# All eleven chunk pairs of the feed-forward layer in seven products, spaced token tile steps, first input chunk in two transfers

## The chip, the core and the metric

The kernel runs on one core of a Trainium2 chip. The metric is the device time of one execution in microseconds (us). Matrix products run on TensorE (PE in the profile; its weight loads are PEld), elementwise work on VectorE (DVE), ScalarE (ACT) and GpSimd (POOL), and transfers are issued from the queues of SyncE (SP), ScalarE and GpSimd. All five run side by side and wait for one another through semaphores; each works through its own instructions in order.

## The reference

A decoder trunk of two layers on 1024 tokens of width 1024, in float32. Each layer adds a mixer (layer 0: dilated attention and forgetting attention side by side; layer 1: differential attention) and then a convolutional gated feed-forward part to the running sum `h`. The part that the change touches most:

```python
def conv_glu_ffn(n, w_up, conv_w, conv_b, w_down):   # n: 1024x1024, D_FF = 2816
    gate, up = jnp.split(n @ w_up, 2, axis=-1)
    gp = jnp.pad(gate, ((0, 0), (CONV_WIDTH - 1, 0), (0, 0)))
    conv = conv_b
    for j in range(CONV_WIDTH):
        conv = conv + gp[:, j:j + s] * conv_w[j]
    return (jax.nn.silu(conv) * up) @ w_down
...
h = h + conv_glu_ffn(rms_norm(h, ffn_norm[l]), ...)
...
return rms_norm(h, final_norm)
```

## The kernel before

Everything is kept transposed: channels lie on the 128 partitions, tokens along the free dimension, in two halves of 512 tokens (`HT`). A float32 product is made of three products of a rounded-down type (`mm3`): each operand is split into a high and a low part (`split`, `wget`), and high x high, high x low and low x high are summed in PSUM. So one "block product" (512 input channels or one 128-channel chunk with four output tiles, 512 tokens) is 12 matmuls of 128x512, or 24 of half the width.

**Feed-forward, up.** The 2816 inner channels are 22 chunks of 128 (`NF`). For each chunk `ffn_up` makes gate and up with Winograd's form of Strassen's scheme, in seven block products (numbered 1 to 7 in `step`) where the plain way has eight. Weight sums for it are made on GpSimd (`plan_ffn`).

**Feed-forward, down.** The down product takes the chunks in pairs (2j, 2j+1). A pair with two output halves (tiles 0 to 3 and 4 to 7) and two token halves is again a 2x2 block product. For the last ten pairs (`NS = 10`) it is done in seven products: the sums of the activations (`td`, four per pair) are made by `close` in `ffn_up` on VectorE, the sums of the weights (`sd`, four per pair) by `sums` on GpSimd, one pair per chunk from chunk 10 (`NH`) on; both go to DRAM and are read back. The first pair is done plainly, in eight products. `ffn_down` runs through the parts that `down_parts` lists: each part is a row of items, an item is one weight tile and one activation tile (two loads, two splits, one block product), and all items of a part are summed in one set of four PSUM banks, `X` or `Y`. There are eight parts with 10, 12, 10, 10, 12, 10, 12 and 2 items, 78 in all. At the end of a part `take` adds the banks to the residual tiles `h`, and where the part is marked done, `after` starts the next norm on them (`after0` in layer 0, `after1` in layer 1). In the last part of layer 1 the last items (`tail`) run in two passes over 256 tokens each, and `after1` calls `finish` (statistics, reciprocal root, spread over the partitions, scaling, output) for each.

**Attention and projections** are woven by `weave`: attention steps are events with planned times, the projections (`jobs`) are generators that yield after each small piece with a cost in planned us. After each event the planner runs the job at hand until its account `done` reaches the event's `goal`. The last job of a mixer is `blocks` in `out_jobs`: nine steps; step m scales token tile m of the first token half (`token_blocks`, VectorE), stores it, and splits tile m-1 (ScalarE, VectorE). Behind each step stand three yields; they run pieces of `rest` (the second token half of the output projection) if the attention unit that it needs is done (`rest.after in self.fins`), and else cost 0.1 each. Afterwards the framework puts each engine's instructions in order by the program's order and by when it reckons them ready.

**Start.** The first 128 input channels (512 KB) come in one transfer on SP's queue behind two weight tiles; `norm_chunk` then works on each token half.

Of the kernel before, what the change touches and what calls it, by code (L numbers as in the profile page):

```python
# [13 lines left out]
ALU = mybir.AluOpType  # L14
# [4 lines left out]
P = 128  # L19
T = 1024  # L20
D = 1024
NK = D // P
HT = 512
NF = 22
# [25 lines left out]
class Trunk:  # L50
# [175 lines left out]
    def norm_a(self, st, c, half, src, gi):  # L226

        nc = self.nc
# [4 lines left out]
        if c == 0:  # L233
            st["acc"][half] = st["acct"](half)
            sq = st["acc"][half]
        else:
            sq = st["sqt"]()
# [3 lines left out]
    def norm_b(self, st, c, half, src, gi, sq):  # L241

        nc = self.nc
# [5 lines left out]
        if c:  # L249
            nc.vector.tensor_tensor(st["acc"][half], st["acc"][half], sq, ALU.add)  # L250
# [582 lines left out]
    NS = 10  # L833
# [47 lines left out]
    def down_parts(self, l):  # L881

        n0 = NF // 2 - self.NS
        A = lambda k, c: self.a["wdown"][l, k][:, c * HT:(c + 1) * HT]
        B = lambda k, t: self.act[l][k][:, t * HT:(t + 1) * HT]
        js = range(n0, NF // 2)
        std = lambda c, t: [(A(k, c), B(k, t)) for k in range(2 * n0)]
# [4 lines left out]
                list(zip(odd(A, 0), odd(B, 0))) + std(0, 0),  # L892
                list(zip(S(2), Tk(2))),
                list(zip(S(3), Tk(3))),
                list(zip(odd(A, 1), Tk(4))) + std(1, 0),
                list(zip(S(1), Tk(1))),
                list(zip(S(4), odd(B, 1))) + std(0, 1),
                std(1, 1)]
# [24 lines left out]
    def ffn_up(self, l, plan, blocks, down):  # L923
# [4 lines left out]
        order, W, _ = plan  # L928
# [69 lines left out]
        def close():  # L998
            tt = nc.vector.tensor_tensor
            while late:  # L1000
# [7 lines left out]
                if j < NF // 2 - self.NS:  # L1008
                    continue
# [16 lines left out]
        def sums(fc, p):  # L1026


            j = NF // 2 - self.NS + fc - self.NH
# [4 lines left out]
            if p == 6:  # L1034
                for x, k, c in (("11", 0, 0), ("21", 0, 1), ("22", 1, 1), ("12", 1, 0)):
                    sw[x] = t()
                    self.put(sw[x], self.a["wdown"][l, 2 * j + k][:, c * HT:(c + 1) * HT])
            elif p == 5:
                tt(sw["11"], sw["11"], sw["21"], ALU.subtract)
                self.store(self.sd[l][j, 3], sw["11"])  # L1040
                nc.gpsimd.dma_start(sw["21"], self.a["wdown"][l, 2 * j + 1][:, HT:], accum_op=ALU.add)
# [39 lines left out]
    def ffn_down(self, l, plan, act, h, after, mid):  # L1081
# [8 lines left out]
        parts = [(X, True, None, False), (X, False, (0, 0), True), (Y, True, (0, 1), False), (Y, False, (4, 1), False),  # L1090
                 (Y, False, (4, 0), True), (X, True, (4, 1), False), (X, False, (0, 1), True), (Y, True, (4, 1), True)]
# [7 lines left out]
        for q, (banks, begin, at, done) in enumerate(parts):  # L1099
            if begin:  # L1100
                ps = [self.pj(t) for t in banks]
            self.pmap["small"] = ["A"] if q == 7 else ["Q"]
            seg = D[q]
            end = len(seg) - min(3, len(seg) - 1)
            lastq = q == 7 and l == 1
# [43 lines left out]
    def run(self):  # L1149
# [29 lines left out]
        def out_jobs(l, w, base):  # L1179
# [24 lines left out]
            def blocks():  # L1204
                rest.fetch()
                more = rest.gen()
                for m in range(9):
# [7 lines left out]
                    for _ in range(3):  # L1215
                        yield next(more, 0.0) if rest.after in self.fins else 0.1
# [69 lines left out]
        for c in range(NK):  # L1286
# [4 lines left out]
            nc.sync.dma_start(xc, a["xT"][c * P:(c + 1) * P, :])  # L1291
# [155 lines left out]
        def after0(m, c):  # L1447
            hf = c.start // HT
            if (m, hf) == (0, 0):
# [69 lines left out]
        def after1(m, c):  # L1519
# [3 lines left out]
            if m == 0:  # L1523
# [139 lines left out]
```

## Time and profile before

| | us |
|---|---|
| three runs, median (lowest to highest) | 2530.19 (2528.14 to 2540.12) |
| the profiled execution | 2523.64 |
| its span, first to last instruction | 2521.9 |
| TensorE busy | 2445.1 |
| VectorE busy | 1976.4 |
| ScalarE busy | 1219.2 |
| GpSimd busy | 702.6 |

The busy time of an engine is the sum of its instructions' times; what is left of the span is time in which the engine had nothing to do or waited. TensorE's instructions overlap by a part (a matmul begins before the one ahead has left the array), so its pace is read from the distance of two starts.

### The profile page before, as it was taken

The page shows a single profiled execution, that of the slowest core. Times are in us where ns is not written, and L with a number is a line of the kernel's source. Part 1 is how long each engine was busy: PE and PEld are TensorE (multiplying, and loading weights), DVE is VectorE, ACT ScalarE, POOL GpSimd, SP SyncE. Part 2 cuts the span into 40 slices and gives each one's busy share as a digit, 9 for nine tenths or more (in the row PEclk, how much of TensorE's full clock was granted, in tenths as well). Part 3 has the DMA queues.
Part 4 walks back from the last instruction along what each step waited for, and adds up shares of the span by engine and source line. Part 5 has one row for each costly group of instructions (what it writes and reads, how often), then busy time and mean ns, then how long its engine had stood idle before and what let it go on. Part 6 is the DMA issues. An engine that isn't in the chain of part 4 may idle for free.

```text
span 2521.9 us, 38243 instructions
## 1 busy us (share of the span) xinstructions
PE 2445.1 (97%) x12511; PEld 2034.3 (81%) x12511; DVE 1976.4 (78%) x3885; ACT 1219.2 (48%) x2443; POOL 702.6 (28%) x930
## 2 busy tenths in 40 slices
PE   8999999999899999999999999999889999999997
PEld 7899898887688888787888888877767888887786
DVE  7778878877988988775666878887888888887655
ACT  5456655555543434453534555555554343445433
POOL 1211112222544665100021111132135366730000
PEclk9999999999999999999999999999999999999998
DMA  5655556756667887664655555586476678856644
GB/s 186 225 168 168 175 166 207 243 201 235 209 190 229 243 253 223 217 219 160 196 194 179 191 166 181 187 284 201 159 256 187 201 242 252 253 184 235 228 136 152
DMA packets 240790, 515.96 MB, mean 205 GB/s; under 512 B 36696, under 2 KB 49616, under 8 KB 240592
## 3 DMA queue, kind: packets, MB, share of 16 engines
q1 hardware_dynamic: 175184, 311.63, 38.9%
q0 software_dynamic: 64832, 201.37, 24.1%
q8 instruction: 99, 1.62, 0.3%
q14 instruction: 99, 0.81, 0.1%
q10 hardware_dynamic: 576, 0.52, 0.1%
HBM read 349.75 MB, written 163.64 MB: 204 GB/s over the span
## 4 chain that ended last, share of the span: by engine, by line
PE 80%; DMA 6%; DVE 6%; issue 4%; ACT 2%; POOL 1%; SPq 0%; ACTq 0%; DVEq 0%; POOLq 0%
PE pj L145 66%; PE D L145 5%; PE O L145 4%; PE T L148 4%; DVE wl L131 1%; PE small L145 1%; DMA wr<-in_wgate 1%; DMA wr<-in_wdown 1%; DMA ar<-act 1%; ACT wh L129 1%; DMA rt<-sr 1%; DMA ar<-td 1%; DVE e L615 1%; DVE bt L166 1%; DVE e L771 0%
## 5 line engine op out<-in xcount | busy, mean ns | idle before, releaser
L145 PE MATMUL pj<-bt,wh 128*128 128x512 f32 x1760 | 552.1, 394 | 7.3 <-DVE bt L166 4.4
L145 PEld LDWEIGHTS pj<-bt,wh 128*128 128x128 f32 x1760 | 330.5, 188 | 85.5 <-DVE bt L166 6.0
L145 PE MATMUL pj<-nh,wh 128*128 128x512 f32 x864 | 354.6, 410 | 17.8 <-ACT nh L232 8.8
L131 DVE TENSOR_TENSOR wl<-wr,wh 128x512 fp32r<-128x512 f32 (+2 forms) x340 | 239.5, 706 | 162.9 <-ACT wh L129 150.8
L145 PE MATMUL pj<-bt,wl 128*128 128x512 f32 x880 | 346.6, 394 | 0.0
L129 ACT ACTIVATE wh<-wr 128x512 fp32r<-128x512 f32 (+2 forms) x340 | 211.6, 624 | 277.4 <-PE pj L145 121.4
L145 PE MATMUL pj<-nl,wh 128*128 128x512 f32 x864 | 343.9, 398 | 0.0
L145 PE MATMUL pj<-nh,wl 128*128 128x512 f32 x864 | 343.2, 397 | 0.0
L131 DVE TENSOR_TENSOR wl<-wq,wh 128x512 fp32r<-128x512 f32 x268 | 274.3, 1025 | 31.9 <-ACT wh L129 31.7
L129 ACT ACTIVATE wh<-wq 128x512 fp32r<-128x512 f32 x268 | 166.8, 628 | 233.8 <-PE pj L145 176.1
L849 POOL TENSOR_TENSOR wq<-wq 128x512 f32<-128x512 f32 x132 | 202.4, 1538 | 213.9 <-DVE wl L131 106.8
L145 PE MATMUL pj<-ah,wh 128*128 128x512 f32 (+1 forms) x628 | 247.7, 395 | 4.8 <-DVE h L1115 3.1
L145 PE MATMUL pj<-al,wh 128*128 128x512 f32 (+1 forms) x628 | 246.0, 392 | 0.0
L145 PE MATMUL pj<-ah,wl 128*128 128x512 f32 (+1 forms) x628 | 245.8, 392 | 0.0
L145 PEld LDWEIGHTS pj<-nh,wh 128*128 128x128 f32 x864 | 164.7, 191 | 51.2 <-ACT sc L956 9.9
L165 ACT ACTIVATE ph<-T 128x512 fp32r<-128x512 f32 (+3 forms) x288 | 139.2, 487 | 129.6 <-PE T L148 127.1
L145 PEld LDWEIGHTS pj<-bt,wl 128*128 128x128 f32 x880 | 165.5, 188 | 39.5
L145 PEld LDWEIGHTS pj<-nh,wl 128*128 128x128 f32 x864 | 164.0, 190 | 37.3
L145 PEld LDWEIGHTS pj<-nl,wh 128*128 128x128 f32 x864 | 164.7, 191 | 30.1 <-DVE nl L247 0.5
L166 DVE TENSOR_TENSOR pl<-T,ph 128x512 fp32r<-128x512 f32 (+3 forms) x288 | 157.7, 552 | 34.8 <-ACT ph L165 33.6
L148 PE MATMUL T<-ident,e 128*128 128x128 f32 x864 | 143.2, 275 | 6.8 <-DVE e L771 4.0
L145 PE MATMUL pj<-wh,nh 128*128 128x256 f32 (+1 forms) x512 | 149.2, 293 | 0.0
(494 smaller groups left out, 5297.8 us busy)
## 6 DMA issues: line engine op xcount, KB each, us to landing
wq<-in_wgate SPq DMA_DIRECT2D x88, 256.0 KB, 4.6
wq<-in_wup SPq DMA_DIRECT2D x88, 256.0 KB, 5.6
act<-v POOLq DMA_DIRECT2D x44, 512.0 KB, 3.4
td<-sc POOLq DMA_DIRECT2D x80, 256.0 KB, 4.5
wq<-in_wdown SPq DMA_DIRECT2D x80, 256.0 KB, 4.5
sd<-wq POOLq DMA_DIRECT2D x80, 256.0 KB, 4.3
ar<-td SPq DMA_DIRECT2D x80, 256.0 KB, 3.7
wr<-sd SPq DMA_DIRECT2D x80, 256.0 KB, 2.9
```

The lines of the kernel that those rows point to most:

```text
L129: nc.scalar.activation(hi[:, :n], raw[:, :n], AF.Copy)
L131: nc.vector.tensor_tensor(lo[:, :n], raw[:, :n], f(hi[:, :n]), ALU.subtract)
L145: self.last = self.nc.tensor.matmul(*args, **kw)
L148: self.last = self.nc.tensor.transpose(*args)
L165: nc.scalar.activation(hi, src, AF.Copy)
L166: nc.vector.tensor_tensor(lo, src, f(hi), ALU.subtract)
L615: self.nc.vector.tensor_tensor_reduce(out=e[:, k0:k0 + w], in0=d[:, :w], in1=in1(k0, w), scale=1.0, scalar=init, op0=ALU.add, op1=ALU.min, ...
L849: nc.gpsimd.tensor_tensor(dst, x, y, op)
```

## The change

Six edits belong together: `NS` becomes 11, so that the first pair of chunks is done in seven products like the others. Its activation sums are made in chunks 0 and 1, and the weight sums, one pair per chunk from chunk 10 on, now reach to chunk 20. `down_parts` has seven parts of 11 items, 77 in all; the eighth part is gone. The two halves of the output tiles change places in all of it, so the tiles 4 to 7 of the first token half come first, and the last two parts both use the banks `X`: part 5 ends the tiles 0 to 3 of the second token half, part 6 goes on in the same banks and ends the tiles 4 to 7. The running sum of the norm starts at the tile that comes first. In `blocks` a step whose `rest` may not run yet costs 2.0 once instead of 0.1 three times. The first input chunk comes in two transfers of 256 KB, one for each token half.

```diff
--- before.py
+++ after.py
@@ -230,7 +230,7 @@
             g = self.gn[:, gi * 8 + c:gi * 8 + c + 1]
             st["h"][c, half] = self.big.tile([P, HT], F32R, name="nh", tag="big")
             nc.scalar.activation(st["h"][c, half], src, AF.Copy, scale=g)
-        if c == 0:
+        if half not in st["acc"]:
             st["acc"][half] = st["acct"](half)
             sq = st["acc"][half]
         else:
@@ -246,7 +246,7 @@
             st["l"][c, half] = self.big.tile([P, HT], F32R, name="nl", tag="big")
             nc.vector.scalar_tensor_tensor(st["l"][c, half], src, g, f(st["h"][c, half]),
                                            ALU.mult, ALU.subtract)
-        if c:
+        if sq is not st["acc"][half]:
             nc.vector.tensor_tensor(st["acc"][half], st["acc"][half], sq, ALU.add)
 
     def norm_chunk(self, st, c, half, src, gi):
@@ -830,7 +830,7 @@
     NH = 10
 
 
-    NS = 10
+    NS = NF // 2
 
     def plan_ffn(self, l):
         a, nc = self.a, self.nc
@@ -880,22 +880,19 @@
 
     def down_parts(self, l):
 
-        n0 = NF // 2 - self.NS
-        A = lambda k, c: self.a["wdown"][l, k][:, c * HT:(c + 1) * HT]
+        A = lambda k, c: self.a["wdown"][l, k][:, (1 - c) * HT:(2 - c) * HT]
         B = lambda k, t: self.act[l][k][:, t * HT:(t + 1) * HT]
-        js = range(n0, NF // 2)
-        std = lambda c, t: [(A(k, c), B(k, t)) for k in range(2 * n0)]
+        js = range(NF // 2)
         S = lambda i: [self.sd[l][j, i] for j in js]
         Tk = lambda i: [self.td[l][j, i] for j in js]
         odd = lambda f, i: [f(2 * j + 1, i) for j in js]
         return [[(A(2 * j, 0), B(2 * j, 0)) for j in js],
-                list(zip(odd(A, 0), odd(B, 0))) + std(0, 0),
+                list(zip(odd(A, 0), odd(B, 0))),
                 list(zip(S(2), Tk(2))),
                 list(zip(S(3), Tk(3))),
-                list(zip(odd(A, 1), Tk(4))) + std(1, 0),
+                list(zip(odd(A, 1), Tk(4))),
                 list(zip(S(1), Tk(1))),
-                list(zip(S(4), odd(B, 1))) + std(0, 1),
-                std(1, 1)]
+                list(zip(S(4), odd(B, 1)))]
 
     def ffn_order(self):
 
@@ -1005,8 +1002,6 @@
                 tt(x[:, h1], y[1], s.pop((fc, 3)), ALU.mult)
                 self.store(self.act[l][fc], x)
                 j = fc // 2
-                if j < NF // 2 - self.NS:
-                    continue
                 if fc % 2 == 0:
                     t1[0] = scratch()
                     tt(t1[0], x[:, h1], x[:, h0], ALU.subtract)
@@ -1026,7 +1021,7 @@
         def sums(fc, p):
 
 
-            j = NF // 2 - self.NS + fc - self.NH
+            j = fc - self.NH
             if fc < self.NH or j >= NF // 2:
                 return
             tt = nc.gpsimd.tensor_tensor
@@ -1034,11 +1029,11 @@
             if p == 6:
                 for x, k, c in (("11", 0, 0), ("21", 0, 1), ("22", 1, 1), ("12", 1, 0)):
                     sw[x] = t()
-                    self.put(sw[x], self.a["wdown"][l, 2 * j + k][:, c * HT:(c + 1) * HT])
+                    self.put(sw[x], self.a["wdown"][l, 2 * j + k][:, (1 - c) * HT:(2 - c) * HT])
             elif p == 5:
                 tt(sw["11"], sw["11"], sw["21"], ALU.subtract)
                 self.store(self.sd[l][j, 3], sw["11"])
-                nc.gpsimd.dma_start(sw["21"], self.a["wdown"][l, 2 * j + 1][:, HT:], accum_op=ALU.add)
+                nc.gpsimd.dma_start(sw["21"], self.a["wdown"][l, 2 * j + 1][:, :HT], accum_op=ALU.add)
             elif p == 7:
                 tt(sw["22"], sw["22"], sw["11"], ALU.subtract)
                 self.store(self.sd[l][j, 2], sw["22"])
@@ -1087,8 +1082,8 @@
         X, Y = ("A", "A", "B", "O"), ("S", "S", "Q", "Q")
         s0, n = [], 0
 
-        parts = [(X, True, None, False), (X, False, (0, 0), True), (Y, True, (0, 1), False), (Y, False, (4, 1), False),
-                 (Y, False, (4, 0), True), (X, True, (4, 1), False), (X, False, (0, 1), True), (Y, True, (4, 1), True)]
+        parts = [(X, True, None, False), (X, False, (4, 0), True), (Y, True, (4, 1), False), (Y, False, (0, 1), False),
+                 (Y, False, (0, 0), True), (X, True, (0, 1), True), (X, False, (4, 1), True)]
 
         def residual(m0, hf):
             for m in range(m0, m0 + 4):
@@ -1099,10 +1094,10 @@
         for q, (banks, begin, at, done) in enumerate(parts):
             if begin:
                 ps = [self.pj(t) for t in banks]
-            self.pmap["small"] = ["A"] if q == 7 else ["Q"]
+            self.pmap["small"] = ["S"] if q == 6 else ["Q"]
             seg = D[q]
             end = len(seg) - min(3, len(seg) - 1)
-            lastq = q == 7 and l == 1
+            lastq = q == 6 and l == 1
 
             def take(m, c):
 
@@ -1212,8 +1207,11 @@
                         hl = (self.big.tile([P, HT], F32R, name=x, tag="big") for x in ("nh", "nl"))
                         st["h"][m - 1, 0], st["l"][m - 1, 0] = hl
                         self.split(st["h"][m - 1, 0], st["l"][m - 1, 0], t0[m - 1])
-                    for _ in range(3):
-                        yield next(more, 0.0) if rest.after in self.fins else 0.1
+                    if rest.after in self.fins:
+                        for _ in range(3):
+                            yield next(more, 0.0)
+                    else:
+                        yield 2.0
                 while rest.after not in self.fins:
                     yield 0.1
                 yield from more
@@ -1288,7 +1286,8 @@
                 xc = f(ap.tile([P, T], F32R, name="KS", tag="KS", bufs=self.kbufs))
             else:
                 xc = ap.tile([P, T], F32, name="e", tag="e", bufs=self.ebufs)
-            nc.sync.dma_start(xc, a["xT"][c * P:(c + 1) * P, :])
+            for o in cs if c == 0 else [slice(0, T)]:
+                nc.sync.dma_start(xc[:, o], a["xT"][c * P:(c + 1) * P, o])
             for half in range(2):
                 self.norm_chunk(st, c, half, xc[:, cs[half]], 0)
             if c in (1, 3):
@@ -1446,7 +1445,7 @@
 
         def after0(m, c):
             hf = c.start // HT
-            if (m, hf) == (0, 0):
+            if (m, hf) == (4, 0):
                 st1["acct"] = st1["sqt"] = lambda half=0: self.fp.tile([P, HT], F32, name="sc", tag="sc",
                                                                        bufs=self.nsc)
             sq = self.norm_a(st1, m, hf, H[0][m, hf], 2)
@@ -1520,7 +1519,7 @@
             hf, w = divmod(c.start, HT)
             o = slice(w, w + c.stop - c.start)
             h = H[1][m, hf][:, o]
-            if m == 0:
+            if m == 4 * (1 - hf):
                 if w == 0:
                     acc[hf] = self.fp.tile([P, HT], F32, name="sc", tag="sc", bufs=self.nsc)
                 nc.scalar.activation(acc[hf][:, o], h, AF.Square)
```

## Rows read from the trace of the kernel before

**Rows 1.** Page, part 1: busy time, share of the span, instructions of each engine.

```profile
PE 2445.1 (97%) x12511; PEld 2034.3 (81%) x12511; DVE 1976.4 (78%) x3885; ACT 1219.2 (48%) x2443; POOL 702.6 (28%) x930
```

**Rows 2.** Waits of TensorE over the span: total us, times, longest us.

```profile
PE pj L145 <- ACT nh L232: 8.8, 1, 8.8
...
PE small L148 <- DVE pl L166: 7.3, 2, 7.1
...
PE pj L145 <- DVE h L1115: 3.1, 4, 1.3
```

**Rows 3.** Windows: busy us (instructions) of PE, PEld, DVE, ACT, POOL; PE clock, DMA share, GB/s.

```profile
672.00:1035.00 363.00, 363.00 (x1565) 294.37 (x1565) 310.96 (x426) 151.55 (x249) 191.55 (x214) 1.00 0.71 221
...
1803.00:1813.00 10.00, 10.00 (x49) 8.43 (x49) 8.78 (x27) 6.56 (x19) 2.01 (x4) 0.79 0.48 155
1813.00:1831.00 18.00, 16.59 (x91) 13.43 (x90) 11.97 (x28) 8.37 (x22) 0.00 (x0) 1.00 0.31 99
...
2268.00:2503.00 235.00, 233.26 (x1022) 188.29 (x1020) 151.91 (x247) 112.01 (x192) 3.24 (x6) 1.00 0.58 193
```

**Rows 4.** Timeline of TensorE in the last part: start us, duration us.

```profile
2491.21 0.40 PE L145 MATMUL pj<-ah,wh 128*128 128x512 f32 x1
2491.45 0.40 PE L145 MATMUL pj<-al,wh 128*128 128x512 f32 x1
...
2500.39 0.28 PE L145 MATMUL pj<-al,wh 128*128 128x256 f32 x1
2500.51 0.28 PE L145 MATMUL pj<-ah,wl 128*128 128x256 f32 x1
```

**Rows 5.** Groups by line and shape: busy us, mean ns, idle before.

```profile
L1022 DVE TENSOR_TENSOR sc<-v,sc 128x512 f32<-128x512 f32 x20 | 29.6, 1478 | 1.7 <-DMA sc<-act 1.6
...
L1017 DVE TENSOR_TENSOR sc<-v,sc 128x512 f32<-128x512 f32 x20 | 13.7, 686 | 0.1
...
L1043 POOL TENSOR_TENSOR wq<-wq 128x512 f32<-128x512 f32 x20 | 32.2, 1612 | 0.0
```

**Rows 6.** Windows of layer 0's up product: chunk 1 closes; chunk 3 closes, with sums.

```profile
700.00:713.00 13.00, 13.00 (x57) 10.52 (x57) 11.82 (x18) 5.26 (x9) 5.04 (x6) 1.00 0.57 179
...
727.00:741.00 14.00, 14.00 (x63) 11.34 (x62) 13.16 (x21) 5.45 (x10) 6.07 (x8) 1.00 0.76 242
```

**Rows 7.** Timeline of VectorE, end of layer 1's attention.

```profile
1793.10 2.08 DVE L1145 SCALAR_TENSOR_TENSOR rt<-rt,gn,rb 128x512 f32<-128x512 f32 x3
...
1802.02 0.69 DVE L166 TENSOR_TENSOR pl<-T,ph 128x512 fp32r<-128x512 f32 x1
...
1810.99 1.29 DVE L771 SCALAR_TENSOR_TENSOR e<-e,cf 128x1024 f32<-128x1024 f32 x1
```

**Rows 8.** Timeline of TensorE, the same stretch.

```profile
1802.76 1.12 PE L148 MATMUL small<-ident,Ra 128*128 128x128 f32 x4 [7.13 <-DVE pl L166]
```

**Rows 9.** Timeline of the start.

```profile
3.86 0.63 ACT L129 ACTIVATE wh<-wr 128x512 fp32r<-128x512 f32 x1 [1.83 <-DMA wr<-in_wqkA]
...
4.81 0.63 ACT L129 ACTIVATE wh<-wr 128x512 fp32r<-128x512 f32 x1 [0.33 <-DMA wr<-in_wqkA]
...
8.06 0.72 ACT L232 ACTIVATE nh<-e,gn 128x512 fp32r<-128x512 f32 x1 [2.62 <-DMA e<-in_xT]
...
8.84 0.80 PE L145 MATMUL pj<-nh,wh 128*128 128x512 f32 x1 [8.84 <-ACT nh L232]
```

**Rows 10.** Timeline of the end.

```profile
2502.31 0.28 PE L145 MATMUL pj<-ah,wl 128*128 128x256 f32 x1
...
2503.63 0.61 PE L145 MATMUL small<-ones,sc 128*128 128x1 f32 x4 [1.05 <-DVE sc L1537]
...
2507.11 1.32 ACT L1530 ACTIVATE sc<-h 128x256 f32<-128x256 f32 x4
...
2507.57 4.00 PE L145 MATMUL small<-ones,sc 128*128 128x1 f32 x18 [0.66 <-ACT sc L1530]
...
2515.11 3.22 DVE L1566 SCALAR_TENSOR_TENSOR y<-h,gn,small 128x256 f32<-128x256 f32 x8 [1.18 <-PE small L145]
```

## The prediction

> **What bounds the kernel.** I began with the busy shares of the page [rows 1]: TensorE works for 97% of the span, the next engine, VectorE, for 78%. So a gain must take matmuls away or close one of the gaps that make up the other 3%. The list of TensorE's waits [rows 2] says which gaps there are: one of 8.8 us that ends with the first product of ScalarE, two of 7.3 us in all (one of them 7.1) behind `pl` on VectorE, four short ones behind `h`. The windows [rows 3] show that the up product of layer 0 has no gap at all (363.00 of 363.00), that the last down product loses 1.7 us of 235, and that the ten us behind the long wait ran at a granted clock of 0.79, a mix of the lower and the higher level. Then I read the timelines at the three places where the edits meet a gap: the end of layer 1's attention [rows 7, 8], the start [rows 9] and the end [rows 10].
>
> **The eighth product.** Before, a layer's down product has 78 items, after it 77; an item is 12 matmuls of 512 columns. Over two layers 24 matmuls go. Their pace is the window's: 363 us for 1565 of them [rows 3], 0.232 us each; two starts in the last part lie as far apart [rows 4]. **24 x 0.232 = 5.6 us less**, and since TensorE is the bound in both down products, all of it is on the path. The tail of the last part had one item in two passes of 256 columns and now has three. That costs nothing: two half-width starts are 0.12 us apart, so two halves take what one whole takes [rows 4].
>
> What the seven products need in return, per layer: four VectorE sums between 686 and 1478 ns [rows 5], so 2.7 to 5.9 us, three GpSimd sums of about 1.61 us (4.8 us), eight stores and six loads of 256 KB. They fall in chunks 0, 1 and 20 of the up product. I cost them at nothing, and the cover is TensorE's own work there: the window in which chunk 1 closes without sums has VectorE busy for 11.82 of 13 us, the one in which chunk 3 closes with the same sums for 13.16 of 14, and TensorE was full in both [rows 6]. Chunk 20 will look like chunks 10 to 19, which lie in the full window [rows 3]. If that cover were gone, at most 5.9 + 4.8 = 10.7 us per layer would come onto the path (the third rival). The sums of the first pair are read back in the third part, tens of us after they are stored, so their transfers wait for nobody. Each layer also saves one item's four splits.
>
> **The order of the parts.** Exchanging the output halves moves the same work. New is only that the finished tiles 0 to 3 of the second token half are followed by a part in the same banks: its first matmuls wait for `take`, and `take` now shares VectorE with the norm. The nearest rows are the waits behind `h`: four, 3.1 us in all, 1.3 at most [rows 2]. The wait could be nothing, since a tail of nine matmuls per tile (2.1 us) gives `take` time; at the other end it is 1.3 us per layer. I take 0.5 per layer, **1 us more** (0 to 2.6). The same change lets the squares of tiles 0 to 3 run a part earlier, off the path as before.
>
> **The token tile steps.** In layer 0 the attention unit that `rest` needs is done before `blocks` begins, by the planner's own order, so both versions yield the same pieces and nothing changes. In layer 1 it is not. I followed the planner's account through the code: `blocks` begins with the account at 249.0, and the marks that follow are 249.3 and 252.3. At 0.1 a yield a step costs 0.3, so all nine steps go out before the second mark is reached. VectorE shows them as one block: from 1793.10 to the `pl` at 1802.02 nearly nothing but token tiles [rows 7]. That `pl` frees the bank for the four transposes of `Ra`, and TensorE stood still for 7.13 us until 1802.76 [rows 8]; over the next ten us the granted clock averaged 0.79 [rows 3].
>
> At 2.0 a step the account passes the same marks thus: step 0 at the first, step 1 at the second, two behind the next row of scores, one and then two more around the last row, and the last two when the unit is done. The planner gives `rest` three pieces before the end of the list in either case, so no matmul moves back. Ahead of that `pl` now stand three VectorE operations of steps 0 and 1, not fourteen. The most that this can give is the whole wait and the lost clock: 7.1 + 10 x (1 - 0.79) = 9.2 us. But VectorE is then the limit: it was busy for 8.78 of the ten us from 1803 on, and the last row's `e` ends at 1812.3 [rows 3, 7]. Of the sixteen operations of the block some three to seven now stand behind that row, at about 0.65 us each: 2 to 4.5 us by which the last unit ends earlier. What TensorE can put into the hole meanwhile is the first two thirds of `rest`, whose inputs are there. The seven late steps also cost VectorE some 9 us further on, where it has 18 - 11.97 = 6.0 us idle [rows 3]; the 3 us that don't fit could make the first block products wait, which is the bound on the other side. So the edit gives between 9.2 less and 3 more; I take **5 us less**, between VectorE's 4.5 and the whole wait, nearer to the first.
>
> SP's queue waits at the store of that unit's statistics row, with the next weights behind it, so those start as much earlier as the unit ends; POOL's queue issues the tile stores in the same order, only wider apart, and the loads of `rest` behind them.
>
> **The first chunk.** TensorE starts at 8.84, when ScalarE has made the first `nh` from 8.06 on [rows 9]; ScalarE was ready from 5.44 (4.81 + 0.63). The two weight tiles of 256 KB ahead of the chunk reached ScalarE at 3.86 and 4.81, 0.95 us apart. A first half of 256 KB at that pace would be there at 5.76: 2.3 us less. If the transfers behind it share the engines evenly, it comes when the whole came: nothing. The second half is needed only after six cold matmuls, and one more issue ahead of the next chunk costs that chunk little, since ScalarE has four operations per chunk to do first. I take **1.5 us less**. The Trainium skill speaks against cutting transfers up: DMA: Bandwidth & Descriptors, section Bandwidth, wants them batched to 1 MiB or more. By the fit that the same page gives for another queue (2.0 us and 436 GB/s) the smaller transfer would be some 0.6 us faster, an estimate by which the sum below would gain 0.9 us less; the weights' rows here come closer together than that.
>
> **The end.** From the start of the last half-width matmul at 2502.31 to the end of the span at 2521.9 are 19.6 us [rows 10]. Before, the second pass of 256 columns was over in 1.4 us, so the statistics of the first pass began only behind it, at 2503.63; the squares of the second pass (L1530) stood on ScalarE behind the spread of the first until 2507.11, and the statistics of the second pass took TensorE 4.00 us at 18 instructions, 0.22 each, where the first four took 0.61, 0.15 each. Now a pass has 36 matmuls, 4.2 us. The statistics of the first pass are ready about 1.3 us after its end (2503.63 - 2502.31 before), take 0.6, and root and spread take 3.5 (2515.11 - 2511.57): its spread is over some 1.2 us behind the last matmul, no longer five. Step by step behind that matmul: spread and squares, 1.5; twenty statistics instructions at 0.15, 3.0; root and spread, 3.5; scaling and stores as before, 2521.9 - 2515.11 = 6.8. That is 14.8, so **4.8 us less**. If the order on the engines stays, it gives nothing; if part of the statistics goes ahead too, 6.
>
> **Sum.** -5.6 + 1.0 - 5.0 - 1.5 - 4.8 = -15.9. The profiled execution took 2523.64 us (1.7 around its span) and would take 2507.7; the median of the runs shown lies 6.5 higher, at 2530.19, which gives **2514.3**. The bounds summed are -23.1 and 0.
>
> **Rivals.** One half of a per cent, 12.65 us, is about what a measurement of this kernel tells from no change.
>
> First, VectorE is the limit at the end of attention, and the wait only moves: the last unit's rows come no earlier, or the late tiles make the first block products of the up product wait. For it speaks VectorE's 8.78 of 10 us, against it the 6.0 us that it has idle right after [rows 3]. The edit gives nothing: -15.9 + 5.0 = -10.9, 2519.3.
>
> Second, the end keeps its order (both passes, then the statistics one after the other), because the framework reckons the root's chain longer than 4.2 us. The change then doesn't do there what its longer tail allows: -15.9 + 4.8 = -11.1, 2519.1.
>
> Third, on the other side: the up product is full only as long as VectorE keeps up, and it has 0.84 us to spare in 14 where a pair is summed [rows 6]. If chunks 0 and 1, with the backlog of the token blocks before them, and chunk 20 go over it, each us over is one of TensorE's; 10.7 us in each layer make +21.4 - 15.9 = +5.5, 2535.7. It decides from 8.0 us per layer on. Against it speaks that ten pairs in each layer passed without a gap. GPSIMD Engine Reference, section Specifications, of the Trainium skill says that GpSimd shares its SBUF interfaces with VectorE when that reads two inputs there; the trace agrees (the same sum took 686 and 1478 ns), and by that rule three more GpSimd sums would make this rival.
>
> **Chances.** Forecast 0.60; first rival 0.18, second 0.15, third 0.07. The limit of half a per cent is at 2517.5. The forecast's own range, 2506 to 2521, has a quarter of its weight beyond it; of the first two rivals, whose times lie just beyond it, two fifths fall short of it; of the third about half would be slower by more than that. So faster 0.45 + 0.13 = 0.58, slower 0.04, same the rest, 0.38. The range, 2505 to 2527, takes in the first two rivals and the bank waits at their worst.
>
> **What would show it.** Right: 628 `ah,wh` matmuls as before, but 24 of them half as wide instead of 8; no `small` wait of 7 us near 1800, token tiles in five or more groups on VectorE; first matmul near 7.3; statistics of the first pass ahead of the last matmul, and 14 to 15 us from that to the end; the up product still full. Wrong: a new wait behind `e`, `nl` or `bt` of several us around 1810 to 1910, a gap in the up product, or an end of 18 us and more.

## The result and the profile after

| | median, us | runs | lowest to highest |
|---|---|---|---|
| before | 2529.16 | 4 | 2527.90 to 2540.12 |
| after | 2508.97 | 4 | 2507.37 to 2512.70 |
| the same kernel timed again beside before | 2511.14 | 6 | 2506.85 to 2513.68 |

The change makes the kernel faster: the ratio to before is 0.9919, with a 95% interval of 0.9902 to 0.9937, and 0.993 (0.9916 to 0.9944) in the second set. 2514.3 were forecast, with 2505 to 2527 as the range. The profiled execution of after took 2508.77 us (span 2507.0), 14.9 less than that of before. The page's first part answers to [rows 1]:

```profile
PE 2436.2 (97%) x12511; PEld 2028.4 (81%) x12511; DVE 1976.4 (79%) x3881; ACT 1216.4 (49%) x2439; POOL 717.7 (29%) x954
```

TensorE is busy for 8.9 us less, and fills the same 97% of a shorter span. The list of its waits, first rows and a later one, beside [rows 2]:

```profile
PE small L145 <- DVE dg L273: 9.5, 5, 3.5
PE pj L145 <- ACT nh L232: 6.5, 1, 6.5
...
PE T L148 <- DVE pl L166: 4.7, 2, 3.1
PE T L148 <- DVE e L771: 4.3, 11, 1.4
...
PE pj L145 <- ACT s L1106: 2.6, 2, 1.4
```

The wait for `small` behind `pl`, 7.1 us long, is gone; a shorter one behind `pl` has come, 3.1, for the transposes `T`. The first wait of all is 2.3 us shorter. No wait behind `h` is left in the list. The costliest row of TensorE's waits in layer 0's down product alone, before and then after:

```profile
PE pj L145 <- DVE h L1115: 2.4, 3, 1.3
```

```profile
PE pj L145 <- ACT s L1106: 1.4, 1, 1.4
```

Now the windows, as [rows 3, 6] give them. Layer 1's attention begins 4.9 us earlier in after (1356.9 for 1361.8), so the two windows at its end are set 5 us earlier than those of [rows 3]; the last window holds layer 1's down product, ten us earlier.

```profile
672.00:1035.00 363.00, 363.00 (x1568) 294.47 (x1567) 317.72 (x431) 151.60 (x249) 201.22 (x226) 1.00 0.74 231
700.00:713.00 13.00, 13.00 (x58) 10.52 (x58) 12.47 (x21) 4.98 (x8) 5.56 (x7) 1.00 0.72 245
...
1798.00:1808.00 10.00, 8.17 (x38) 6.34 (x37) 8.99 (x16) 5.99 (x12) 3.23 (x6) 0.84 0.56 185
...
1808.00:1826.00 18.00, 15.30 (x78) 12.54 (x77) 12.26 (x28) 7.57 (x20) 1.07 (x2) 0.97 0.48 162
...
2262.00:2493.00 231.00, 229.05 (x1033) 186.24 (x1031) 147.60 (x247) 110.22 (x194) 3.32 (x7) 1.00 0.59 193
```

The up product of layer 0 is still full, though VectorE works 6.8 us more in it and GpSimd 9.7. Chunk 1 (700 to 713) now makes sums too, and TensorE stays full (13.00). At the end of attention the granted clock of the ten us from 1798 on is 0.84; the ten us behind the long wait had 0.79 before, so little of the clock came back with the wait. In the 18 us behind these VectorE is busy for 12.26, so the late token tiles haven't filled the room that it had there (11.97 before).

The groups of matmuls by shape show 604 + 24 = 628 `ah,wh` products, with 24 half as wide:

```profile
L145 PE MATMUL pj<-ah,wh 128*128 128x512 f32 x604 | 237.8, 396 | 3.2 <-ACT s L1106 2.6 <-DVE v L1001 0.6
...
L145 PE MATMUL pj<-ah,wh 128*128 128x256 f32 x24 | 6.8, 285 | 0.0
```

VectorE's timeline at the end of layer 1's attention, the token tiles and the last row's `e` ([rows 7]):

```profile
1785.99 1.41 DVE L1140 SCALAR_TENSOR_TENSOR rt<-rt,gn,rb 128x512 f32<-128x512 f32 x2
...
1790.89 0.73 DVE L1140 SCALAR_TENSOR_TENSOR rt<-rt,gn,rb 128x512 f32<-128x512 f32 x1
...
1797.91 0.75 DVE L1140 SCALAR_TENSOR_TENSOR rt<-rt,gn,rb 128x512 f32<-128x512 f32 x1
...
1802.75 1.28 DVE L771 SCALAR_TENSOR_TENSOR e<-e,cf 128x1024 f32<-128x1024 f32 x1
```

and TensorE's waits of a us and more there ([rows 8]):

```profile
1793.93 0.55 PE L148 MATMUL T<-ident,e 128*128 128x128 f32 x3 [3.11 <-DVE pl L166]
1795.94 0.80 PE L145 MATMUL D<-KS,QS 128*128 128x512 f32 x1 [1.07 <-DVE mn L615]
...
1804.18 1.06 PE L148 MATMUL T<-ident,e 128*128 128x128 f32 x8 [1.41 <-DVE e L771]
```

The block has become seven groups between 1785.99 and 1801.32, and 7.13 us of waiting in one piece have become 3.11 + 1.07 + 1.41 = 5.6 in three. The last row's `e` starts 8.2 us earlier (1802.75 for 1810.99); 4.9 us of that are attention's earlier beginning, so attention itself gains 3.3 up to there.

The start ([rows 9]): ScalarE takes the first `nh` almost without a wait (0.1 us), for its half of the chunk has landed.

```profile
4.94 0.63 ACT L129 ACTIVATE wh<-wr 128x512 fp32r<-128x512 f32 x1 [0.44 <-DMA wr<-in_wqkA]
...
5.71 0.72 ACT L232 ACTIVATE nh<-e,gn 128x512 fp32r<-128x512 f32 x1
...
6.48 0.80 PE L145 MATMUL pj<-nh,wh 128*128 128x512 f32 x1 [6.48 <-ACT nh L232]
```

The end ([rows 10]), three timelines; TensorE:

```profile
2488.05 0.28 PE L145 MATMUL pj<-ah,wl 128*128 128x256 f32 x1
2488.50 0.61 PE L145 MATMUL small<-ones,sc 128*128 128x1 f32 x4 [0.17 <-DVE sc L1536]
2488.96 0.36 PE L145 MATMUL pj<-ah,wh 128*128 128x256 f32 x1
...
2491.18 0.28 PE L145 MATMUL pj<-ah,wh 128*128 128x256 f32 x1
2491.42 0.71 PE L145 MATMUL small<-dg,ones 128*128 128x128 f32 x4
2491.89 0.36 PE L145 MATMUL pj<-al,wh 128*128 128x256 f32 x1
...
2492.44 0.28 PE L145 MATMUL pj<-ah,wl 128*128 128x256 f32 x1
2492.56 2.76 PE L145 MATMUL small<-ones,sc 128*128 128x1 f32 x20
2498.82 1.19 PE L145 MATMUL small<-dg,ones 128*128 128x128 f32 x4 [3.50 <-DVE dg L273]
```

VectorE, in the root of the first pass and of the second:

```profile
2490.30 0.15 DVE L183 TENSOR_TENSOR rq_z<-rq_y 128x2 f32<-128x2 f32 x1
...
2495.36 0.16 DVE L178 TENSOR_SCALAR rq_x<-small 128x2 f32<-128x2 f32 x1 [2.18 <-PE small L145]
2496.03 0.77 DVE L183 TENSOR_TENSOR rq_z<-rq_y 128x2 f32<-128x2 f32 x1 [0.51 <-ACT rq_y L182]
2496.82 0.65 DVE L184 TENSOR_TENSOR rq_z<-rq_z,rq_x 128x2 f32<-128x2 f32 x1
2497.50 0.65 DVE L185 TENSOR_SCALAR rq_z<-rq_z 128x2 f32<-128x2 f32 x1
```

and GpSimd:

```profile
2492.63 5.50 POOL L1563 TENSOR_TENSOR y<-y,sc 128x256 f32<-128x256 f32 x8 [212.20 <-ACT sc L1555]
```

Statistics and spread of the first pass now run among the products of the second (the last product starts at 2492.44), and the twenty statistics behind it follow 0.12 us behind its start. To the end of the span it is 14.5 us, for 19.6. The same root operation takes 0.15 us at 2490.30 and 0.77 at 2496.03, when GpSimd is scaling.

### The profile page after: what moved, and what is told of

Its sections match the earlier page's. It is cut to its first block, busy times and chain, and to the rows that moved or that the text cites. A ratio compares the mean times of both kernels' runs of the same rounds, so it can differ in the third digit from the quotient of the medians.

```text
span 2507.0 us, 38271 instructions
## 1 busy us (share of the span) xinstructions
PE 2436.2 (97%) x12511; PEld 2028.4 (81%) x12511; DVE 1976.4 (79%) x3881; ACT 1216.4 (49%) x2439; POOL 717.7 (29%) x954
## 4 chain that ended last, share of the span: by engine, by line
PE 80%; DVE 7%; DMA 6%; issue 4%; ACT 2%; POOL 1%; SPq 0%; DVEq 0%; ACTq 0%; POOLq 0%
PE pj L145 67%; PE D L145 5%; PE O L145 4%; PE T L148 4%; DMA wr<-in_wgate 1%; DVE wl L131 1%; DMA wr<-in_wdown 1%; PE small L145 1%; DVE bt L166 1%; ACT wh L129 1%; DVE e L615 1%; DMA ar<-act 1%; ACT e L764 0%; DVE e L771 0%; DMA wr<-in_wqkC 0%
## 5 line engine op out<-in xcount | busy, mean ns | idle before, releaser
L131 DVE TENSOR_TENSOR wl<-wr,wh 128x512 fp32r<-128x512 f32 (+2 forms) x338 | 234.1, 694 | 149.6 <-ACT wh L129 136.8
```

The source lines that it names most:

```text
L131: nc.vector.tensor_tensor(lo[:, :n], raw[:, :n], f(hi[:, :n]), ALU.subtract)
```

## The experiments

Each was timed beside the kernel before. The code cuts show only the lines that change. "After" has the ten runs of the table above.

**The parts taken back, one at a time.** First the kernel after unchanged, then with the old `blocks` steps, with the first chunk in one transfer, and with a tail of one item in the last part:

```diff
 # old steps
+                    for _ in range(3):
+                        yield next(more, 0.0) if rest.after in self.fins else 0.1
 # one transfer
+            nc.sync.dma_start(xc, a["xT"][c * P:(c + 1) * P, :])
 # tail of one item
+            end = len(seg) - (1 if lastq else min(3, len(seg) - 1))
```

> The changed kernel itself, timed again beside the kernel before. The profiled executions lie 14.9 us apart (2523.6 and 2508.8), the medians of the first runs 20.2. If the sum of the prediction (15.9) is the true size, the ratio is 0.9937 or so; if the profiled execution of before was only a quick one, it is 0.992.

> The changed kernel with the token tile steps as before (0.1 three times). Theory, that the block of sixteen VectorE operations held the transposes back: a wait of 6 to 8 us comes back before the transposes of Ra near 1790 and the time is 4 to 6 us above the changed kernel. Rival, that VectorE is the limit there and the wait only moved: within 1.5 us of it, though the long wait is back.

> The changed kernel with the first input chunk in one transfer. Theory: the first matmul starts near 8.8 again, not 6.5, and the time is 1.4 to 2.4 us above the changed kernel. Rival, that the first us are made good by later waits for weights and stores anyway: first matmul at 8.8, but the time within 0.7 us.

> The changed kernel with a last tail of one item in place of three (12 half-width matmuls a pass). Theory, that the length of the pass puts the first statistics ahead of the last matmul: the end grows from 14.5 to about 19 us behind the last product of the down part, the time rises by 4 to 5 us. Rival, that the end gained because the last part now shares its banks with the one before, or by the clock: no more than 1.5 us.

| | median, us | lowest to highest | ratio to before |
|---|---|---|---|
| after again | 2511.14 | 2506.85 to 2513.68 | 0.9930 (0.9916 to 0.9944) |
| old steps | 2512.58 | 2511.56 to 2513.52 | 0.9935 (0.9923 to 0.9947) |
| one transfer | 2509.34 | 2509.16 to 2510.94 | 0.9924 (0.9911 to 0.9937) |
| tail of one | 2514.48 | 2514.19 to 2517.70 | 0.9946 (0.9933 to 0.9958) |

After again lies between the two ratios that were expected, and its interval holds both. Against it, the steps are worth 1.4 us, the transfer nothing that shows, the tail 3.3. By the medians, then, steps and transfer fall to the rivals of their expectations, and the tail falls short of its 4 to 5; but the intervals overlap, so by the times alone no one of them is settled. The traces tell more. With the old steps the long wait is back, as in [rows 8]:

```profile
1797.79 1.12 PE L148 MATMUL small<-ident,Ra 128*128 128x128 f32 x4 [7.13 <-DVE pl L166]
```

With the chunk in one transfer ScalarE waits for it again, and TensorE starts 1.63 us later than after, at 8.11 where 8.8 was expected:

```profile
7.34 0.72 ACT L232 ACTIVATE nh<-e,gn 128x512 fp32r<-128x512 f32 x1 [1.40 <-DMA e<-in_xT]
...
8.11 0.80 PE L145 MATMUL pj<-nh,wh 128*128 128x512 f32 x1 [8.11 <-ACT nh L232]
```

With one item in the tail, four and two statistics instructions run behind the last product, and the other eighteen have the old length of 4.00 us:

```profile
2497.27 0.42 PE L145 MATMUL small<-ones,sc 128*128 128x1 f32 x2
2498.26 4.00 PE L145 MATMUL small<-ones,sc 128*128 128x1 f32 x18 [0.56 <-ACT sc L1529]
```

**One part alone.** The kernel before with the new steps and nothing else; the kernel after with steps, transfer and tail all taken back, so that the eleventh pair and the new order are left; and the kernel before with one pair fewer.

```diff
 # only the steps, on before
+                    else:
+                        yield 2.0
 # nine pairs, on before
-    NS = 10
+    NS = 9
```

> The kernel before with the token tile steps at 2.0 a yield, nothing else. Theory: the wait of 7 us behind pl near 1800 goes, the clock stays up, and the last unit ends earlier; 4 to 5 us less at the first block product of layer 1's output and at the end, about 2524.5; ratio 0.998. Rival: the gain at that place is given back before the up product's first matmul or at the end (the step alone, taken back from the kernel after, cost 1.4 to 3.6 us in the medians): 1 to 2 us less.

> The kernel after with the three other edits taken back: old token tile steps, the first chunk in one transfer, a tail of one item in the last part. Left are the eleventh pair and the order of the parts. Theory: 5.6 us of matmuls less, and layer 0's down product loses about 2.5 us of short waits besides, as every version with the new order showed; 6 to 8 us less than before, ratio 0.997. Rival, the prediction's own terms: 5.6 less and 1 more by waits for the banks, 4.6 us less, ratio 0.998. Second rival: the parts don't add up, and the products alone bring 10 us or more, or 2 us or less.

> The kernel before with one pair fewer in seven products (nine pairs, two pairs plain), nothing else. Theory: a pair is worth its 24 matmuls of the two layers, 24 x 0.232 = 5.6 us, and its sums are hidden under the up product, so this is 5.6 us slower than before (4.5 to 7), about 2535; ratio 1.002. Rival: the sums cost the up product something, so that a pair is worth clearly less: 0 to 3 us slower. Second rival: each of the plain pair's waits costs as well, as layer 0's part seemed to show (5.9 us for one layer alone): 9 us and more slower.

| | median, us (runs) | before there (runs) | ratio to before |
|---|---|---|---|
| only the steps | 2525.68 (11) | 2527.91 (23) | 0.9986 (0.9975 to 0.9997) |
| only products and order | 2517.89 (9) | 2527.12 (17) | 0.9965 (0.9952 to 0.9977) |
| nine pairs | 2531.98 (12) | 2527.91 (23) | 1.0014 (1.0003 to 1.0025) |

The steps alone bring 2.2 us by the medians and 3.5 (0.8 to 6.3) by the ratio: between the 4 to 5 of the theory and the 1 to 2 of the rival, with an interval that holds both. Products and order bring 9 us (5.8 to 12.1 by the interval), more than the prediction's 4.6, which lies outside. Nine pairs cost about 4 us (0.8 to 6.3), but that run doesn't measure a pair cleanly, which its expectation overlooked: the last part then has four items, so its tail has three by itself, and its end is 15.3 us instead of 19.6.

**The stages of all profiled executions.** One execution of the kernel before took 2521.48 us and another 2540.12, a difference larger than any term here, so a stage is better compared over all traces. From TensorE's timelines: the start of layer 0's up product (first matmul on `bt`, its summed inputs); layer 0's down product (first to last start of a matmul on `ah` or `al`, the high and low part of an activation tile); layer 1 from its first transposes `T` to the first `bt`; layer 1's down product; from the start of the last product to the end of the span. All in us.

| kernel | up 0 starts | down 0 | attention 1 | down 1 | end |
|---|---|---|---|---|---|
| before | 652.94 | 223.28 | 528.68 | 221.10 | 19.56 |
| only steps | 653.07 | 222.94 | 524.68 | 222.70 | 19.80 |
| nine pairs | 656.21 | 225.21 | 526.56 | 226.11 | 15.28 |
| only products | 652.87 | 219.38 | 528.48 | 218.54 | 20.34 |
| old steps | 652.06 | 216.53 | 530.20 | 219.85 | 14.53 |
| after | 651.57 | 217.37 | 524.36 | 220.00 | 14.53 |
| after again | 650.71 | 217.10 | 522.65 | 222.75 | 14.54 |
| one transfer | 652.96 | 215.90 | 524.89 | 220.68 | 14.56 |
| tail of one | 651.06 | 219.14 | 523.31 | 219.41 | 20.21 |
| tail of four | 652.97 | 216.51 | 524.73 | 222.29 | 13.57 |
| tail of five | 652.15 | 216.62 | 527.64 | 221.89 | 12.32 |
| one sum more | 651.79 | 215.84 | 525.38 | 219.86 | 14.53 |
| weight sums more | 652.57 | 216.71 | 524.60 | 218.33 | 14.52 |
| both kinds more | 652.90 | 217.66 | 523.19 | 219.27 | 13.81 |

Ten pairs in the old order have 223.1 in layer 0's down product on average, the eleven kernels in the new order 217.2 (none above 219.4). Old steps have 528.5 in attention, new ones 524.5, with one of ten (527.64) among the old. The split chunk starts the up product at 652.0 on average, the whole one at 653.0 (without the kernel of nine pairs, at 656.21), and the two sets touch. The first matmul itself starts at 6.4 to 6.7 us in five of the nine traces with two transfers and at 7.6 to 8.3 in the other four, 7.2 on average; with one transfer it starts at 8.1 to 9.5, 8.9 on average.

**A longer tail.** Five and four items in place of three, for a shorter end:

```diff
+            end = len(seg) - (5 if lastq else min(3, len(seg) - 1))
```

> The kernel after with a tail of five items in the last part instead of three. Theory: the first pass ends 4.2 + 5.6 = 9.8 us ahead of the last matmul's end instead of 4.2, so its scaling on GpSimd (5.5 us) and its root are over before the second pass needs VectorE for its own root; the root's small operations there take 0.16 us again instead of 0.65 to 0.77, which is 1.6 us, and the end is about 13 us behind the last matmul instead of 14.5: 1 to 2 us less than the kernel after. Rival: the second pass's chain is set by its own twenty statistics and its output alone, and the GpSimd work only moves: within 0.5 us of after at the end.

> The kernel after with a tail of four items. A tail of five ended 12.3 us behind the last product instead of 14.5, but lost 1.5 us around 2482 to 2485, where five items' operands were wanted at once. Theory: four items keep most of the gain at the end (13 us behind the last product) and lose nothing there: about 1 us less than after in the profile, too little for the medians to tell. Rival: the wait for the operands comes with four items too, or the end stays at 14.5: no gain.

Five: 2513.13 us (2511.98 to 2519.95), ratio 0.9945 (0.9932 to 0.9959). Four: 2509.40 (2504.60 to 2515.94), 0.9931 (0.9915 to 0.9948). With five items GpSimd is done before the root's middle operations, and they are short again. GpSimd's timeline, then VectorE's:

```profile
2496.07 5.59 POOL L1563 TENSOR_TENSOR y<-y,sc 128x256 f32<-128x256 f32 x8 [210.49 <-ACT sc L1555]
```

```profile
2502.51 0.16 DVE L183 TENSOR_TENSOR rq_z<-rq_y 128x2 f32<-128x2 f32 x1 [0.51 <-ACT rq_y L182]
2502.71 0.16 DVE L184 TENSOR_TENSOR rq_z<-rq_z,rq_x 128x2 f32<-128x2 f32 x1
```

So the theory of the end holds, 2.2 us for five items and 1.0 for four. But the down product pays: the distances of TensorE's starts show gaps that three items don't have, together 1.5 us between 2482 and 2485 with five, and 0.9 near 2484 with four. Neither beats after; no better version came out of it.

**How much the up product bears.** The third rival said that the sums run over VectorE's room. Three kernels that add work to after were to show where it decides: one activation sum of each pair done twice on VectorE; two weight sums done again forwards and back on GpSimd (four more per pair); and the latter with three activation sums done twice, which was run first.

```diff
 # one sum more
+                for _ in range(2):
+                    tt(t4, x[:, h0], t2, ALU.subtract)
 # weight sums more, and the same for "12", "22"
                 tt(sw["11"], sw["11"], sw["21"], ALU.subtract)
+                tt(sw["11"], sw["11"], sw["21"], ALU.add)
+                tt(sw["11"], sw["11"], sw["21"], ALU.subtract)
```

> The kernel after with one of the four activation sums of each pair (the last but one, 0.68 us) done twice on VectorE, in all eleven pairs. Theory: VectorE had 0.84 us to spare in the 14 us in which a pair is summed, and 0.68 us still fits: TensorE stays full in the up product, within 2 us of after. Rival: there is no such room, and each of these sums shows in full on TensorE: 11 x 0.68 x 2 = 15 us slower than after.

> The kernel after with two of the weight sums of each pair done again forwards and back on GpSimd (four more sums, some 6 us per pair), and no more work on VectorE. Theory: of the 55 us that the kernel with both kinds of additional sums lost, VectorE's own additional sums made nearly all; GpSimd is idle for half of the window, so here TensorE stays full, within 4 us of after. Rival: GpSimd's sums slow VectorE's by sharing its way to SBUF (0.68 against 1.44 us), and that is what took TensorE's time: 15 to 40 us slower than after.

> The kernel after with three of the four activation sums of each pair done twice on VectorE (about 3 us more per pair) and two of GpSimd's weight sums of each pair done again forwards and back (four sums, 6.4 us more per pair), in all eleven pairs; the results are the same up to rounding. Theory: VectorE has 52 us idle in the 363 us of the up product's window and its queue evens out a burst; 11 x 3 = 33 us fit, TensorE stays full in that window, and the time is within 3 us of after. Rival: the 0.84 us to spare where a pair is summed is the limit, and each us over it is TensorE's: about 2 us per pair, 20 per layer, 40 us slower.

| | median, us | ratio to before | up 0, up 1, us |
|---|---|---|---|
| after | 2508.97, 2511.14 | 0.9919, 0.9930 | 392.33, 391.18 |
| one sum more | 2513.05 | 0.9939 (0.9923 to 0.9955) | 393.21, 391.65 |
| weight sums more | 2533.17 | 1.0033 (1.0021 to 1.0045) | 407.44, 402.40 |
| both kinds more | 2566.05 | 1.0149 (1.0131 to 1.0166) | 421.00, 418.35 |

(Up: first `bt` to first `ah` matmul.) One sum more fits by the up products, which are as long as in after again (393.35 and 391.71); its median is 1.9 us above after again and 4.1 above the first set, too little for these times to settle. The theories of the other two fell. Both kinds together cost 55 us where at most 3 were expected, and the weight sums alone 22 to 24 where at most 4 were: GpSimd's sums, on an engine that had 162 of 363 us idle, cost TensorE 15.1 and 11.2 us in the two up products. The same window of layer 0 as above in that kernel, and TensorE's wait in that up product:

```profile
672.00:1035.00 363.00, 350.86 (x1501) 281.63 (x1501) 342.99 (x412) 143.49 (x238) 263.21 (x267) 1.00 0.72 223
```

```profile
PE pj L145 <- DVE sc L968: 12.1, 10, 2.7
```

VectorE is busy for 25 us more with 19 instructions fewer. The groups by shape in that window say which have grown; the kernel with more weight sums first, after second:

```profile
L131 DVE TENSOR_TENSOR wl<-wq,wh 128x512 fp32r<-128x512 f32 x124 | 172.4, 1397 | 1.8 <-ACT wh L129 1.7
...
L968 DVE TENSOR_TENSOR sc<-sc,pj 128x512 f32<-128x512 f32 x20 | 13.6, 678 | 0.4 <-PE pj L145 0.3
```

```profile
L131 DVE TENSOR_TENSOR wl<-wq,wh 128x512 fp32r<-128x512 f32 x130 | 136.8, 1054 | 16.5 <-ACT wh L129 16.5
...
L968 DVE TENSOR_TENSOR sc<-sc,pj 128x512 f32<-128x512 f32 x21 | 14.3, 679 | 1.7 <-PE pj L145 1.6
```

The weight split, which reads two SBUF tiles (`wq`, `wh`), went from 1054 to 1397 ns; the sum that reads a PSUM bank (`pj`) kept its 679. The split's 0.343 us x 124 = 42.5 us nearly fill the 363 - 317.7 = 45.3 us that VectorE had idle there in after, and TensorE waited 12.1 us in that up product, in ten waits of at most 2.7, about one per pair. Counted over this kernel's whole trace, none of the 407 weight splits of this shape beside which no elementwise operation of GpSimd ran took more than 0.70 us, and the 152 that one overlapped by 0.3 us or more took 1.83 on average. One instruction shows it by itself: of the same splits, the one that starts together with a GpSimd sum takes 2.15 us, the next one 0.69. VectorE's timeline of the kernel with more weight sums, then GpSimd's:

```profile
726.38 2.15 DVE L131 TENSOR_TENSOR wl<-wq,wh 128x512 fp32r<-128x512 f32 x1
...
730.49 0.69 DVE L131 TENSOR_TENSOR wl<-wq,wh 128x512 fp32r<-128x512 f32 x1
```

```profile
726.38 1.59 POOL L849 TENSOR_TENSOR wq<-wq 128x512 f32<-128x512 f32 x1
```

GPSIMD Engine Reference, section Specifications, of the Trainium skill names this sharing, for VectorE instructions with two SBUF inputs; the rows agree.

## Why the prediction came out right

**The products and the banks** were forecast as 5.6 less and 1.0 more; products and order alone brought 9 us (5.8 to 12.1). The matmuls are as reckoned: with a tail of one item on both sides, layer 1's down product shrank from 221.9 (two traces) to 219.0 (two traces), 2.9, for 12 x 0.232 = 2.8. The term that was mis-sized is the banks: layer 0's down product shrank by 5.9, so 3.2 more than its matmuls, where 0.5 more waiting had been put. The wait that this 0.5 stood for, at the start of part 6, is in none of the eleven traces of the new order. In the profiled pair, gaps between starts in layer 0's down product went from 4.3 us to 1.6 (two of before's, 0.92 and 1.50 near 1136 and 1139, have no like in after). They are waits behind `h` at the start of part 3. Behind `h` TensorE waited 2.4, 1.4 and 1.8 us there in the three traces of the old order (parts 3 and 6), and in the new order not at all in eight traces of eleven and 0.3 to 0.9 us in three. The wait behind `s` at the start of part 1 stands in both orders, between 0 and 2.0 us. Why the new order avoids most of the waits behind `h` was not tried out.

**The steps**, 5 less forecast: 4.0 in the stage table, 3.5 by the run alone. The place and the cause were right: taking back this edit brought the 7.13 us wait back, and all four traces with old steps have it. The first rival (the wait only moves, nothing gained) held for a part: 5.6 of the 7.1 us stand in after as three shorter waits, behind `pl`, `mn` and `e` (the 3.1 behind `pl` in all ten traces with new steps, further ones of 1.1 to 1.4 in five), and the clock that the upper bound counted as regained was still down, 0.84. The forecast let the last unit end 2 to 4.5 us earlier; from attention's first transposes to the last row's `e` it is 448.5 us on average with old steps and 447.2 with new ones, 1.3 less. The other 2.7 of the 4.0 come behind that row, where no run takes them apart.

**The first chunk**, 1.5 less forecast. The first matmul came 2.4 earlier in the profiled pair, at the most that was allowed for, and 1.7 over all traces; by the up product some 1.0 was left, a difference no larger than the spread of the single traces, and in the times it doesn't show. A gain in the total is not shown.

**The end**, 4.8 less forecast. It is 5.5 shorter (14.4 for 20.0 on average), but the first pass's statistics and spread, now ahead of the last product, push products apart: in after two starts that are otherwise 0.12 us apart lie 0.91 apart around the one and 0.71 around the other. The down product is 1.1 longer on average (220.1 for 219.0), so 4.4 net. The second rival (the order stays) is excluded by the trace, and with a tail of one item the end is 20.2 again in the new order, so the gain is the longer tail's. The steps behind the last product went otherwise than listed, and cancelled: the statistics took 2.76 instead of 3.0 and started at once, while the root's operations behind GpSimd cost 1.6 us more than their 0.16 each.

**The third rival** didn't come about here: both up products kept their length (392.3 and 391.2 us for 392.4 and 390.7), and VectorE still had 45.3 us idle in the full window. Its mechanism is real, but not with the price that it was given. It added up the durations of both engines' sums. In fact GpSimd's sums cost as much as they slow VectorE: 11 x 4 more of them cost 15.1 us in layer 0, while one VectorE sum more per pair, 0.68 us within the 0.84 to spare, cost nothing that shows. The 1478 ns that the prediction set beside 686 are a mean of such cases: that sum of before took 0.68 to 0.69 us where no elementwise operation of GpSimd ran beside it, and 1.3 to 2.1 where one did.

**The total.** The stage means give -1.0 - 5.9 - 4.0 - 1.8 - 5.5 = -18.2, of which the stretch between layer 0's last product and layer 1's first transposes, longer by 0.8 on average (94.0 to 94.8), takes a little back; -15.9 was forecast. Products and banks brought 4.2 us more than their terms (8.8 for 4.6), the steps, the first chunk and the end 1.0, 0.5 and 0.4 less than theirs: part of the nearness of the sum is luck, errors that cancel. The forecast of 2514.3 is the median of before, 2530.19, less that sum, and came out 5.3 us too high. Of these, 1.0 lies in before itself (its median is 2529.16 with a fourth run, and 2527.91 over all 55 on record), and 4.3 in the change, which the medians put at 20.2 in this set and at 17.8 in the second. That the 2507.7 of the profiled execution lies only 1.3 from the median of after is chance too: the execution of before that it starts from (2523.64) was among the quickest.

## What to carry to other kernels

Before work goes to an idle engine, look which instructions of the busy one get longer beside it, as the splits of two SBUF tiles did here: price the work by how much longer those get, not by the idle engine's own time. When one execution varies by more than an edit is worth, cut every trace at the same few instructions and compare stage by stage over all of them; the sums over the stages told what single medians could not. And take a forecast change off the median of many runs of the version before, for one profiled execution can lie 5 us away from it.

## What had not been expected of the hardware

GpSimd multiplying at 128x256 slows operations of VectorE on two columns from 0.16 to between 0.65 and 0.77 us, though there is next to nothing to move in them. In after that holds also for one that reads a single SBUF tile (L185, 0.65 for 0.17), while one that reads PSUM (L178, at 2495.36) kept its 0.16 in the same stretch. And the granted clock fell after the same wait in one execution and not in another. Near the start of layer 1's projections TensorE waits for `dg` in both, 1.84 us in after and 1.85 in before; it did the same eight small products next, and then these are the windows of after and of before behind it:

```profile
1276.50:1280.00 3.50, 3.50 (x20) 3.50 (x19) 1.59 (x5) 1.69 (x4) 1.10 (x2) 0.53 0.57 200
```

```profile
1283.80:1287.30 3.50, 3.50 (x32) 3.50 (x31) 1.59 (x5) 1.70 (x4) 0.97 (x2) 1.00 0.55 167
```

At 0.53, nearly all of it at the lower of the two levels (1.2 GHz), 20 matmuls went through instead of 32: some 1.4 us (12 x 0.12) that no edit here explains. Why it fell in the one and not in the other stays open.
